# A chunked RWKV-7 recurrence under dense matmuls: turned keys made one step earlier and in another PSUM ring, six receptance buffers, a block inversion in less SBUF

## The chip, the cores and the metric

The kernel runs on one core of a Trainium2 chip. That core has a matrix engine (TensorE, here PE), a vector engine (VectorE, DVE), a scalar engine (ScalarE, ACT), a general engine (GpSimd, POOL) and a queue engine (SyncE, SP) that issues the DMAs. Each engine works through its own list of instructions in order and waits at semaphores for the others. The metric is the device time of one execution in microseconds (us); a lower one is better. Before the change the median of three runs is 2755.4 us (2751.41 to 2757.46).

## The reference

The program is a two-layer encoder trunk on one sequence of 1024 tokens with 1024 channels, all in float32:

- layer 0: RWKV-7 time mixing. Six shifted mixes of the input are projected (r, k, v, a decay, a rate a, a gate g). Per head of 64 channels (16 heads) a 64x64 state is carried over all tokens: `state = state*w + (state·a)⊗b + v⊗k`, and the output is `state·r`. Group norm per head, a bonus term, the gate and the output matrix `wo` follow.
- a layer norm of `alpha*x + f(x)`, then a squared-ReLU MLP (1024 to 4096 to 1024), and a layer norm again.
- layer 1: a diagonal complex state-space layer (S5) with GELU and a gated linear unit, layer norm, a second MLP, layer norm.

Only the recurrence of layer 0 is touched by the change.

## The kernel before

**Tiling.** The 1024 tokens are two halves H of 512. Dense layers keep activations as eight tiles of 128 channels x 512 tokens. Every dense product is made of three float32r matmuls (high x high, high x low, low x high; `mm3`), because each operand is split into a high and a low part (`split`: ACT casts, DVE subtracts). The results go to PSUM tiles named `d`. In what follows a *block matmul* is one matmul into a `d` tile, most of them 128x512.

**The recurrence.** It is computed in chunks of 64 tokens by matmuls. There are eight units m = 0..7: unit m is half of the heads (q = m % 2) over 256 tokens, that is four chunks. A unit goes through

- `elem` (L488 on): loads r, k, decay and rate, makes the scaled receptances `AR` (tag `AR`, two tiles a unit, ring of `ARB` = 5) and scaled keys `KB` (two tiles, ring of 2), with small matmuls `pss`, `pn`, `pb` into the PSUM ring `a` (pool `pa`, two buffers);
- `amat` (L563): 32 matmuls `pA` of `KB` with `AR`, also into ring `a`, which DVE masks into the chunk matrices `AT`;
- `kbtrans` (L586): the keys turned, 16 transposes on PE into four PSUM tiles `pT` of ring `c` (pool `pc`, two buffers), which ACT copies to four tiles `kbt` (ring of `KTB` = 4, all of them one unit's);
- `invert` (L598): inverts the unit triangular 64x64 blocks of `AT`. ACT copies the diagonal 32x32 blocks to `blk`, DVE turns them into `xa` (L615), 30 pairs of small DVE instructions substitute forward in PSUM (`xh`), and 32 + 32 small matmuls `pv` with an ACT copy between them (L636, L640, L644) make the off-diagonal part. The result is `XT` (ring of 2);
- `chain` (L662): two halves of two chunks each. A chunk is a step of four matmul groups that wait for one another through ACT and DVE: `pR`, `pX`, `pU` (which uses `kbt`), `pO`. 32 steps make the whole sequence. `pR` to `pO` lie in ring `c`;
- `gnorm` (L713): group norm, bonus and gate, with four transposes `py` in ring `c`, and the store of y.

**Order.** All of it is one straight program. `core` (L767) gives each part a rank, and a list scheduler places the instructions of all engines by rank, by the readiness that it reckons with, and by free buffers. The result is a fixed list per engine. Block matmuls of the projections, of `wo(0)` and of the first MLP have late ranks and fill PE between the steps of the recurrence. A ring of two buffers means that a third tile's first writer waits until the first tile's last reader is done.

**Around it.** `rwkv_proj(0)` and `rwkv_proj(1)` are the projections of the two halves, `wo(0)` follows, then the first layer norm (`layer_norm` from L829: column means `pm`, eight subtractions of `pm` from `hA` on DVE (L852), squares on ACT summed by DVE and POOL (L860), `pq`, the root in `rs` (L866, L867), `rb`, `pr`, eight products (L875), ACT, split). The MLP of half 0 can begin only behind that layer norm. `wo(1)` comes after twelve blocks of that MLP.

Of the kernel before, what the change touches and what calls it, by code (L numbers as in the profile page):

```python
# [33 lines left out]
LN8R = 400000  # L34
MIXR = 100
W0B = 5
ARB = 5
GB = (2, 3, 4)
GV = True

AEN = (0, 0, 0, 0)
# [29 lines left out]
def trunk(ctx, tc, A):  # L71
# [513 lines left out]

    def kbtrans(D):  # L586
        D.kbt = {}
        for j in range(2):
            for c2 in range(2):
                p = pc.tile([128, 2, 2, 128], F32, tag="c", name="pT")  # L590
                for cc in range(2):
                    for i in range(2):
                        PE.transpose(p[:, cc, i], D.KB[j][:, 4 * i + 2 * c2 + cc].rearrange("p j l -> p (j l)"), ident)
                t = kp.tile([128, 2, 2, 128], F32, tag="kbt", name="kbt", bufs=KTB)
                S.copy(t, p)
                D.kbt[j, c2] = t

    def invert(D):  # L598


        at = D.at
        xa = kp.tile([128, 32, 32], F32, tag="xa", name="xa", bufs=1)
        x1 = kp.tile([128, 2, 16, 32], F32, tag="x1", name="x1", bufs=1)
        tmp = x1[:, 0].rearrange("p u j -> p (u j)")
        blk = x1[:, 1]

        xh = pl.tile([128, HT], F32, tag="l", name="xh")
        xv = xh.rearrange("p (t j) -> p t j", t=32)
        xt = kp.tile([128, 16, L], F32, tag="XT", name="XT", bufs=2)
        D.xt = xt  # L610
        for h in range(2):
            for q in range(2):
                r = slice(64 * h + 32 * q, 64 * h + 32 * q + 32)
                S.copy(blk[r].rearrange("p (c i) j -> p c i j", i=NP), at[r, h, :, :, 0, 32 * q : 32 * q + 32])
        V.transpose(xa.rearrange("p t (e u) -> p t e u", e=2),  # L615
                    blk.rearrange("p u t -> p t u").unsqueeze(2).broadcast_to([128, 32, 2, 16]))

        S.mul(xv, xa[:, :, 0:32:2], emask[:, 0:1])
        V.scalar_tensor_tensor(xv, xa[:, :, 1:32:2], emask[:, 1:2], xv, op0=ALU.mult, op1=ALU.add)
        for s in range(1, 31):  # L620
            nt, w = 31 - s, (s + 1) // 2
            tv = tmp[:, 0 : nt * w].rearrange("p (t j) -> p t j", t=nt)
            V.tensor_mul(tv, xa[:, s + 1 : 32, s : s + 1].broadcast_to([128, nt, w]),
                         xv[:, s : s + 1, 0:w].broadcast_to([128, nt, w]))
            V.tensor_add(xv[:, s + 1 : 32, 0:w], xv[:, s + 1 : 32, 0:w], tv)
        for e in range(2):
            d = xh[:, 16 * e : 16 * e + 496 : 33]
            V.tensor_scalar(d, d, emask[:, e : e + 1], None, op0=ALU.add)
        V.transpose(x1[:, 0].rearrange("p u (j e) -> p j e u", e=2), xv.rearrange("p t j -> p j t"))
        V.transpose(xt.rearrange("p u (e t) -> p u e t", e=2),  # L630
                    x1[:, 0].unsqueeze(2).broadcast_to([128, 16, 2, 32]))
        pv1 = pl2 = pl.tile([128, HT], F32, tag="l", name="pv1").rearrange("p (u j) -> p u j", u=16)
        for u in range(16):
            for h in range(2):
                r0 = 64 * h
                PE.matmul(pv1[r0 + 32 : r0 + 64, u], at[r0 : r0 + 32, h, u // NP, u % NP, 0, 32:64],  # L636
                          x1[r0 : r0 + 32, 0, u], start=True, stop=True)
        for h in range(2):
            r0 = 64 * h
            S.copy(x1[r0 + 32 : r0 + 64, 0], pv1[r0 + 32 : r0 + 64])  # L640
        for u in range(16):
            for h in range(2):
                r0 = 64 * h
                PE.matmul(pl2[r0 : r0 + 32, u], x1[r0 + 32 : r0 + 64, 0, u],  # L644
                          xt[r0 + 32 : r0 + 64, u, 32:64], start=True, stop=True)
        for h in range(2):
            r0 = 64 * h
            S.copy(xt[r0 : r0 + 32, :, 32:64], pl2[r0 : r0 + 32])
            G.memset(xt[r0 + 32 : r0 + 64, :, 0:32], 0.0)

        for j in range(2):
            for h in range(2):
                hs = slice(64 * h, 64 * h + 64)
                (S.copy if AEN[2 * j + h] == 0 else G.tensor_copy)(
                    at[hs, h, :, 2 * j : 2 * j + 2, 0], D.AR[j][hs, :, 0].rearrange("p (i c) l -> p c i l", i=2))
# [116 lines left out]
    def core():  # L772
# [5 lines left out]
            cur = elem(0)  # L778
        with rank(5000):
            amat(cur)  # L780
            invert(cur)
        with rank(100000):
            run(pg)
        last = None
        for m in range(8):
# [7 lines left out]
                with rank(LN1R):  # L793
                    first_out.append(layer_norm(first_out[0], 0, 0))
            base = m * 10000
            with rank(base + RK[0]):
                kbtrans(cur)
            nxt = None
            if m < 7:
                with rank(base + RK[1]):  # L800
# [9 lines left out]
            if nxt and m < 6:  # L810
                with rank(base + RK[3]):
                    amat(nxt)
            with rank(base + RK[4]):
                chain(cur, 1)
            with rank(base + RK[5]):
                gnorm(cur, 0)
            if nxt:
                with rank(base + RK[6]):
                    if m == 6:
                        amat(nxt)  # L820
                    invert(nxt)
            last, cur = cur, nxt
        with rank(base + 8000):
# [556 lines left out]
```

## Time and profile before

| | before |
|---|---|
| median of three runs | 2755.4 us (2751.41 to 2757.46) |
| the profiled execution's own time | 2756.91 us |
| its span, first to last instruction | 2755.1 us |
| PE busy | 2602.8 us, 94% of the span |
| DVE / ACT / POOL busy | 1811.4 / 1156.3 / 628.2 us |
| mean granted TensorE clock | 0.958 |
| DMA, bytes moved | 345.90 MB |

Times in the profile are microseconds, engines are named as above, and L12 is line 12 of the kernel before. "Idle before" is how long an engine stood still ahead of an instruction, with what ended that wait behind an arrow. PEclk is the share of full speed that the chip granted to TensorE: 1.0 is 2.4 GHz and 0.5 is 1.2 GHz. Matmuls overlap in the records, so the step from one start to the next tells more of their cost than the duration.

### The profile page before, as it was taken

The page shows a single profiled execution, that of the slowest core. Times are in us where ns is not written, and L with a number is a line of the kernel's source. Part 1 is how long each engine was busy: PE and PEld are TensorE (multiplying, and loading weights), DVE is VectorE, ACT ScalarE, POOL GpSimd, SP SyncE. Part 2 cuts the span into 40 slices and gives each one's busy share as a digit, 9 for nine tenths or more (in the row PEclk, how much of TensorE's full clock was granted, in tenths as well). Part 3 has the DMA queues.
Part 4 walks back from the last instruction along what each step waited for, and adds up shares of the span by engine and source line. Part 5 has one row for each costly group of instructions (what it writes and reads, how often), then busy time and mean ns, then how long its engine had stood idle before and what let it go on. Part 6 is the DMA issues. An engine that isn't in the chain of part 4 may idle for free.

```text
span 2755.1 us, 43773 instructions
## 1 busy us (share of the span) xinstructions
PE 2602.8 (94%) x16582; PEld 2099.3 (76%) x16582; DVE 1811.4 (66%) x3191; ACT 1156.3 (42%) x2038; POOL 628.2 (23%) x515
## 2 busy tenths in 40 slices
PE   7999879899899999889999999999999999999997
PEld 5778767678777877667877788778778887788886
DVE  7477676477788767997658554574765546855556
ACT  7455574554453333344432332344223324433333
POOL 3120642341334212332122000120220001210101
PEclk9989979899879999999999999999999999999999
DMA  4765455465222334564233533233343332333333
GB/s 146 234 206 164 153 180 153 148 192 170 87 79 83 99 94 145 138 157 140 89 123 118 185 96 98 83 89 106 113 164 112 98 96 85 115 96 97 97 94 103
DMA packets 215058, 345.90 MB, mean 126 GB/s; under 512 B 21184, under 2 KB 75584, under 8 KB 214848
## 3 DMA queue, kind: packets, MB, share of 16 engines
q1 hardware_dynamic: 214848, 343.10, 40.2%
q8 instruction: 131, 2.15, 0.3%
q14 instruction: 79, 0.65, 0.1%
HBM read 279.06 MB, written 63.96 MB: 125 GB/s over the span
## 4 chain that ended last, share of the span: by engine, by line
PE 63%; DVE 12%; DMA 5%; issue 4%; ACT 2%; POOL 1%; SPq 0%; ACTq 0%; DVEq 0%; POOLq 0%
PE d L188 53%; DVE wlo L149 2%; DMA wraw<-in_mw_dram 2%; PE py L1234 1%; PE pA L580 1%; PE py L1239 1%; DMA yl<-s_y 1%; DVE hA L975 1%; PE pbu L1190 1%; PE pu L154 1%; PE pR L687 1%; PE pX L692 0%; POOL rl L959 0%; ACT whi L148 0%; DVE t L1202 0%
## 5 line engine op out<-in xcount | busy, mean ns | idle before, releaser
L148 ACT CAST whi<-wraw 128x512 fp32r<-128x512 f32 x668 | 413.6, 620 | 932.0 <-PE d L188 625.0
L149 DVE TENSOR_TENSOR wlo<-wraw,whi 128x512 fp32r<-128x512 f32 x668 | 497.8, 746 | 432.6 <-ACT whi L148 412.7
L188 PE MATMUL d<-qbuf,whi 128*128 128x512 f32 (+1 forms) x2112 | 655.0, 393 | 20.5 <-DVE hA L975 7.7
L188 PEld LDWEIGHTS d<-qbuf,whi 128*128 128x128 f32 x2112 | 390.7, 190 | 115.2 <-DVE hA L975 14.6
L188 PE MATMUL d<-qbuf,wlo 128*128 128x512 f32 (+1 forms) x1056 | 409.5, 390 | 9.5 <-DVE wlo L149 9.3
L188 PE MATMUL d<-oAh,whi 128*128 128x512 f32 (+1 forms) x960 | 394.4, 414 | 21.0 <-ACT ev L417 8.4
L959 POOL TENSOR_TENSOR rl<-rl 128x512 f32<-128x512 f32 x128 | 155.7, 1216 | 1084.4 <-ACT rl L958 1080.4
L188 PE MATMUL d<-oAl,whi 128*128 128x512 f32 (+1 forms) x960 | 390.6, 408 | 5.6 <-DVE oAl L149 5.6
L188 PE MATMUL d<-oAh,wlo 128*128 128x512 f32 (+1 forms) x960 | 390.2, 407 | 5.8 <-DVE wlo L149 3.4
L188 PE MATMUL d<-oBh,whi 128*128 128x512 f32 x704 | 278.6, 396 | 0.0
L188 PE MATMUL d<-oBh,wlo 128*128 128x512 f32 x704 | 277.7, 395 | 0.0
L188 PE MATMUL d<-oBl,whi 128*128 128x512 f32 x704 | 276.4, 393 | 0.0
L188 PEld LDWEIGHTS d<-qbuf,wlo 128*128 128x128 f32 x1056 | 200.0, 190 | 55.1 <-DVE wlo L149 13.6
L188 PEld LDWEIGHTS d<-oAh,whi 128*128 128x128 f32 (+1 forms) x960 | 188.0, 196 | 66.5 <-ACT ev L417 10.2
L188 PEld LDWEIGHTS d<-oAh,wlo 128*128 128x128 f32 (+1 forms) x960 | 188.2, 196 | 49.9 <-DVE wlo L149 5.1
L188 PEld LDWEIGHTS d<-oAl,whi 128*128 128x128 f32 (+1 forms) x960 | 188.4, 196 | 46.9 <-DVE oAl L149 7.8
L975 DVE TENSOR_TENSOR hB<-hB,d 128x512 f32<-128x512 f32 (+1 forms) x256 | 165.2, 651 | 70.7 <-PE d L188 67.9
L975 DVE TENSOR_TENSOR hA<-hA,d 128x512 f32<-128x512 f32 x240 | 162.3, 683 | 47.1 <-PE d L188 44.2
L188 PEld LDWEIGHTS d<-oBh,wlo 128*128 128x128 f32 x704 | 132.5, 188 | 32.1 <-issue 2.0
L188 PEld LDWEIGHTS d<-oBl,whi 128*128 128x128 f32 x704 | 132.6, 188 | 29.9 <-issue 0.9
L188 PEld LDWEIGHTS d<-oBh,whi 128*128 128x128 f32 x704 | 132.8, 189 | 28.2 <-issue 0.7
L149 DVE TENSOR_TENSOR qbuf<-rl,qbuf 128x512 fp32r<-128x512 f32 x128 | 95.7, 748 | 73.0 <-ACT qbuf L148 72.6
(373 smaller groups left out, 3818.1 us busy)
## 6 DMA issues: line engine op xcount, KB each, us to landing
wraw<-in_mw_dram SPq DMA_DIRECT2D x520, 256.0 KB, 2.7
wraw<-in_glu_dram SPq DMA_DIRECT2D x64, 256.0 KB, 2.6
low<-wlo SPq DMA_DIRECT2D x52, 256.0 KB, 2.7
wlo<-low SPq DMA_DIRECT2D x52, 256.0 KB, 3.5
wraw<-in_wk_dram SPq DMA_DIRECT2D x32, 256.0 KB, 3.6
wraw<-in_wr_dram SPq DMA_DIRECT2D x32, 256.0 KB, 3.6
wraw<-in_wv_dram SPq DMA_DIRECT2D x32, 256.0 KB, 4.2
yl<-s_y SPq DMA_DIRECT2D x32, 256.0 KB, 3.1
```

The source lines that it names most:

```text
L148: S.copy(hi, src)
L149: (e or V).tensor_sub(lo, src, hi.bitcast(F32))
L154: PE.matmul(out, x, idt, start=True, stop=True)
L188: bulk.append((PE.matmul(p, w, x, **kw).ins, x.shape[-1]))
L580: PE.matmul(pp[h][:, cc, i], D.KB[j][hs, u].rearrange("p j l -> p (j l)"), D.AR[j][hs, u].rearrange("p j l -> p (j l)"), start=True, stop= ...
L687: hop.append(PE.matmul(pR[hs, i], at[:, h, c, i, 0], vsa[:, cl, h, i], start=True, stop=True))
L959: G.tensor_mul(r, r, r)
L975: V.tensor_add(z, z, p)
L1190: PE.matmul(p[qs, g2, ri], tb[:, g2, ri, qs], u[:, 2 * g2 + par], start=True, stop=True)
L1234: PE.matmul(p[64 * j : 64 * j + 64, g2], ug[f][:, 2 * g2 + par], tv[:, par, g2], start=g2 == 0, stop=False, skip_group_check=True)
L1239: PE.matmul(p[64 * j : 64 * j + 64, g2], hb[qs, 4 * f + g2, ri, 0:NSC], tcm[qs, g2, ri], start=False, stop=ri == 1, skip_group_check=True)
```

## The change

Four things are edited.

1. `kbtrans` is called for the *next* unit, right behind its `amat`, with a rank of `base + 2500`; before, it was called for the current unit at the top of the loop. Its PSUM tiles come from ring `a` and no longer from ring `c`, and its loops run over the chunk pair first.
2. `ARB` goes from 5 to 6.
3. `GB` becomes empty: `gnorm(last, 1)` is traced behind `chain(cur, 0)` for all units, where it was traced ahead of it for m = 2, 3, 4.
4. In `invert` the tile `xa` (4 KB in each partition) goes; the first turned form lies in the unit's own `XT` tile, which is now taken at the beginning of the inversion. `blk` and `tmp` share one tile of 2 KB where `x1` had 4 KB.

An `AR` tile has 4 KB in each partition, so the SBUF use falls by 2 KB.

```diff
-ARB = 5
-GB = (2, 3, 4)
+ARB = 6
+GB = ()
...
     def kbtrans(D):
         D.kbt = {}
-        for j in range(2):
-            for c2 in range(2):
-                p = pc.tile([128, 2, 2, 128], F32, tag="c", name="pT")
+        for c2 in range(2):
+            for j in range(2):
+                p = pa.tile([128, 2, 2, 128], F32, tag="a", name="pT")
...
-        xa = kp.tile([128, 32, 32], F32, tag="xa", name="xa", bufs=1)
-        x1 = kp.tile([128, 2, 16, 32], F32, tag="x1", name="x1", bufs=1)
-        tmp = x1[:, 0].rearrange("p u j -> p (u j)")
-        blk = x1[:, 1]
+        x1 = kp.tile([128, 16, 32], F32, tag="x1", name="x1", bufs=1)
+        tmp = x1.rearrange("p u j -> p (u j)")
+        blk = x1
...
         xt = kp.tile([128, 16, L], F32, tag="XT", name="XT", bufs=2)
         D.xt = xt
+        xa = xt.rearrange("p u j -> p (u j)").rearrange("p (t j) -> p t j", t=32)
...
         with rank(5000):
             amat(cur)
+            kbtrans(cur)
             invert(cur)
...
-            with rank(base + RK[0]):
-                kbtrans(cur)
             nxt = None
...
             if nxt and m < 6:
                 with rank(base + RK[3]):
                     amat(nxt)
+                with rank(base + 2500):
+                    kbtrans(nxt)
...
                 with rank(base + RK[6]):
                     if m == 6:
                         amat(nxt)
+                        kbtrans(nxt)
                     invert(nxt)
```

The scheduler makes another order of it on every engine. From the last step of the recurrence on, the lists of all engines are the same again. Three places in the lists follow, each as the program lists it (line, operation, written tile, read tiles, shape, and how many stand in a row). In the changed kernel the lines of `invert`, `chain` and `gnorm` are shifted by one, those of the layer norm by three.

PE at the first layer norm, before: from the second `pm` matmul (the mean, with the last of the eight columns) on. `pn`, `pb`, `pR` to `pO` and `pA` are the recurrence, and `pq` is the layer norm's sum of squares.

```order
L850 MATMUL pm<-hA,ones_c 128x512
L528 MATMUL pn<-ident,sq 128x128 x4
L557 MATMUL pb<-rksel,kf 64x1 x10
L687 MATMUL pR<-vsa,AT_7087 64x64 x8
L557 MATMUL pb<-rksel,kf 64x1 x6
L692 MATMUL pX<-o,XT 64x64 x8
L580 MATMUL pA<-AR,KB 128x128 x8
L697 MATMUL pU<-vsa,kbt 64x64 x8
L706 MATMUL pO<-st,AR 64x64 x8
L708 MATMUL pO<-vsa,AT_7087 64x64 x8
L580 MATMUL pA<-AR,KB 128x128 x3
L864 MATMUL pq<-ones_c,sq_7814 128x1
```

And PE at the same place of the changed program:

```order
L853 MATMUL pm<-hA,ones_c 128x512
L580 MATMUL pA<-AR,KB 128x128
L593 MATMUL pT<-ident,KB 128x128 x4
L580 MATMUL pA<-AR,KB 128x128 x3
L688 MATMUL pR<-vsa,AT_7082 64x64 x8
L593 MATMUL pT<-ident,KB 128x128 x4
L693 MATMUL pX<-o,XT 64x64 x8
L593 MATMUL pT<-ident,KB 128x128 x8
L698 MATMUL pU<-vsa,kbt 64x64 x8
L707 MATMUL pO<-st,AR 64x64 x8
L709 MATMUL pO<-vsa,AT_7082 64x64 x8
L520 MATMUL pss<-hsel,sq 128x2
```

Twenty-eight of the 32 `pA` of a unit have moved to the front of the layer norm, among the block matmuls of `wo(0)`; four are left behind the mean, and the unit's 16 `pT` now stand there.

DVE at the same layer norm, before: from the eight subtractions of the mean on.

```order
L852 TENSOR_TENSOR hA<-hA,pm 128x512 x8
L529 TENSOR_TENSOR kk<-kk,pn 128x512
L734 TENSOR_REDUCE vr<-osq 128x8
L559 COPY bo<-pb 128x2x4
L860 TENSOR_TENSOR sq_7814<-sq_7814,sq 128x512
L693 COPY vsa<-pX 64x256
L546 SCALAR_TENSOR_TENSOR AR<-kk,E 128x8x64
L735 TENSOR_SCALAR vr<-vr 128x8
L860 TENSOR_TENSOR sq_7814<-sq_7814,sq 128x512
L551 TENSOR_TENSOR KB<-lda,ldsg 64x8x64 x2
L583 TENSOR_TENSOR AT<-pA,amask 128x2x256 x2
L860 TENSOR_TENSOR sq_7814<-sq_7814,sq 128x512
```

And DVE at the same place of the changed program:

```order
L855 TENSOR_TENSOR hA<-hA,pm 128x512 x8
L583 TENSOR_TENSOR AT<-pA,amask 128x2x256
L863 TENSOR_TENSOR sq_7836<-sq_7836,sq 128x512
L694 COPY vsa<-pX 64x256
L550 TENSOR_TENSOR KB<-kf,ldsg 64x8x64 x2
L863 TENSOR_TENSOR sq_7836<-sq_7836,sq 128x512
L616 STREAM_TRANSPOSE XT<-x_8413 128x1024
L863 TENSOR_TENSOR sq_7836<-sq_7836,sq 128x512
L701 TENSOR_TENSOR st<-pU,st 128x256
L702 TENSOR_TENSOR st<-st,PL 128x256
L729 TENSOR_REDUCE sm<-o 128x8
L730 TENSOR_SCALAR sm<-sm 128x8
```

Before, fourteen more instructions stand between the last of these rows and the one that writes `rs` (L866): two state updates, a copy of the state, a scan, a receptance product, a copy, two `AT` products and the rest of two group norms. In the changed program three stand there (L731, L764, L522).

PE at the end of the r projection of half 1, before: `pv` (L636, L644) is the off-diagonal part of an inversion, `pss` and `pn` are the two matmul groups of the key norm. The first fence is at the gate (unit 2's inversion), the second at the values of half 1 (unit 4).

```order
L636 MATMUL pv_3585<-x_3511,AT 32x32 x32
L593 MATMUL pT<-ident,KB 128x128 x8
L644 MATMUL pv_3585<-XT,x_3511 32x32 x32
L593 MATMUL pT<-ident,KB 128x128 x2
L557 MATMUL pb<-rksel,kf 64x1 x16
L520 MATMUL pss<-hsel,sq 128x2 x3
```

```order
L520 MATMUL pss<-hsel,sq 128x2 x4
L593 MATMUL pT<-ident,KB 128x128 x4
L762 MATMUL py<-ident,o 128x2x64 x4
L188 MATMUL d<-oAh,whi 128x512
L188 MATMUL d<-oAl,whi 128x512
L188 MATMUL d<-oAh,wlo 128x512
L528 MATMUL pn<-ident,sq 128x128 x4
L557 MATMUL pb<-rksel,kf 64x1 x16
```

And PE at these two places of the changed program:

```order
L637 MATMUL pv_3610<-x_3536,AT 32x32 x32
L580 MATMUL pA<-AR,KB 128x128 x4
L188 MATMUL d<-oAh,wlo 128x512
L188 MATMUL d<-oAh,w2st 128x512
L580 MATMUL pA<-AR,KB 128x128 x4
L688 MATMUL pR<-vsa,AT 64x64 x5
L580 MATMUL pA<-AR,KB 128x128 x4
L645 MATMUL pv_3610<-XT,x_3536 32x32 x32
L688 MATMUL pR<-vsa,AT 64x64 x3
L580 MATMUL pA<-AR,KB 128x128 x16
```

```order
L580 MATMUL pA<-AR,KB 128x128 x8
L188 MATMUL d<-oAh,whi 128x512
L188 MATMUL d<-oAl,whi 128x512
L188 MATMUL d<-oAh,wlo 128x512
L580 MATMUL pA<-AR,KB 128x128 x4
L593 MATMUL pT<-ident,KB 128x128 x16
L188 MATMUL d<-whi,oAh 128x256
```

The transposes that stood between the two `pv` groups are replaced by `pA`, two block matmuls and part of a `pR`. At the second place `pss` and `pn` are no longer three block matmuls apart, and all 16 `pT` of a unit stand in one piece behind its last `pA`.

## Rows read from the trace of the kernel before

**Rows 1.** The page's first part: busy time, share of the span, instructions

```profile
PE 2602.8 (94%) x16582; PEld 2099.3 (76%) x16582; DVE 1811.4 (66%) x3191; ACT 1156.3 (42%) x2038; POOL 628.2 (23%) x515
```

**Rows 2.** Busy time in three stretches: PE, PEld, DVE, ACT, POOL, PEclk, DMA

```profile
95.00:850.00 755.00, 687.22 (x6229) 569.34 (x6230) 530.27 (x1077) 395.58 (x734) 254.76 (x207) 0.88 0.49 153
740.00:780.00 40.00, 30.99 (x249) 26.44 (x247) 37.08 (x55) 17.18 (x33) 24.93 (x20) 0.56 0.22 66
850.00:1050.00 200.00, 199.51 (x1532) 159.83 (x1533) 141.24 (x266) 73.68 (x138) 41.95 (x36) 1.00 0.31 96
```

**Rows 3.** Waits of PE, 0 to 1050 us: total us, times, longest

```profile
PE pA L580 <- DVE AT L583: 6.4, 3, 3.3
PE pn L528 <- ACT sq L525: 5.1, 3, 3.0
PE pv L644 <- ACT x L640: 3.6, 1, 3.6
PE pb L557 <- POOL kf L552: 3.4, 5, 1.8
PE pT L593 <- ACT kbt L595: 1.0, 1, 1.0
```

**Rows 4.** Timeline of PE at the layer norm: start us, us, engine, line

```profile
722.93 0.60 PE L593 MATMUL pT<-ident,KB 128*128 128x128 f32 x4
723.29 0.49 PE L188 MATMUL d<-oAh,whi 128*128 128x512 f32 x1
...
743.07 0.68 PE L692 MATMUL pX<-o,XT 64*64 64x64 f32 x16 [0.34 <-ACT o L689]
746.12 3.09 PE L580 MATMUL pA<-AR,KB 64*128 64x128 f32 x16 [2.37 <-DVE kk L529]
...
778.49 1.22 PE L188 MATMUL d<-oAh,whi 128*128 128x512 f32 x2 [0.91 <-ACT oAh L148]
```

**Rows 5.** Timeline of DVE at the layer norm

```profile
740.60 4.87 DVE L852 TENSOR_TENSOR hA<-hA,pm 128x512 f32<-128x512 f32 x8 [0.36 <-PE pm L850]
...
746.65 1.31 DVE L860 TENSOR_TENSOR sq<-sq,sq 128x512 f32<-128x512 f32 x1
...
752.08 1.38 DVE L551 TENSOR_TENSOR KB<-lda,ldsg 64x512 f32<-64x512 f32 x2
753.49 1.29 DVE L583 TENSOR_TENSOR AT<-pA,amask 128x512 f32<-128x512 f32 x2
...
762.76 0.69 DVE L730 TENSOR_TENSOR o<-o,sm 128x512 f32<-128x512 f32 x1
...
765.36 0.16 DVE L866 TENSOR_SCALAR rs<-pq 128x4 f32<-128x4 f32 x1
...
773.21 4.87 DVE L875 TENSOR_TENSOR hA<-hA,pr 128x512 f32<-128x512 f32 x8 [0.17 <-PE pr L872]
```

**Rows 6.** Timeline of POOL at the layer norm

```profile
746.15 1.26 POOL L547 TENSOR_TENSOR lda<-kk,lda 128x512 f32<-128x512 f32 x1 [0.73 <-DVE kk L529]
...
780.98 1.65 POOL L523 TENSOR_TENSOR rn<-rn,mhalf 128x8 f32<-128x8 f32 x1
```

**Rows 7.** Tiles xa and kbt: duration ns min/median/max, first and last start

```profile
L615 DVE STREAM_TRANSPOSE xa<-x x8: 1934/2034/2120, 155.5 to 931.3; 128x1024 f32<-128x1024 f32 x8
L595 ACT COPY kbt<-pT x32: 567/587/597, 182.5 to 922.7; 128x512 f32<-128x512 f32 x32
```

**Rows 8.** Timeline of PE where half 1's values begin

```profile
589.35 0.66 PE L528 MATMUL pn<-ident,sq 128*128 128x128 f32 x4 [3.02 <-ACT sq L525]
```

**Rows 9.** All waits of the span: total us, times, longest

```profile
DVE AR L545 <- DMA ldr<-s_r: 22.4, 8, 6.4
```

**Rows 10.** Tiles oBh and st: first users, last step; columns as in rows 7

```profile
L188 PE MATMUL d<-oBh,whi x704: 387/394/632, 1133.5 to 2701.3; 128*128 128x512 f32 x176
L706 PE MATMUL pO<-st,AR x512: 218/218/366, 257.2 to 1046.1; 64*64 64x64 f32 x171
```

More of the change, by code (lines that the diff above doesn't have):

```diff
@@ L628, in invert @@
             V.tensor_scalar(d, d, emask[:, e : e + 1], None, op0=ALU.add)
-        V.transpose(x1[:, 0].rearrange("p u (j e) -> p j e u", e=2), xv.rearrange("p t j -> p j t"))
+        V.transpose(x1.rearrange("p u (j e) -> p j e u", e=2), xv.rearrange("p t j -> p j t"))
         V.transpose(xt.rearrange("p u (e t) -> p u e t", e=2),
-                    x1[:, 0].unsqueeze(2).broadcast_to([128, 16, 2, 32]))
+                    x1.unsqueeze(2).broadcast_to([128, 16, 2, 32]))
         pv1 = pl2 = pl.tile([128, HT], F32, tag="l", name="pv1").rearrange("p (u j) -> p u j", u=16)
@@ L636, in invert @@
                 PE.matmul(pv1[r0 + 32 : r0 + 64, u], at[r0 : r0 + 32, h, u // NP, u % NP, 0, 32:64],
-                          x1[r0 : r0 + 32, 0, u], start=True, stop=True)
+                          x1[r0 : r0 + 32, u], start=True, stop=True)
         for h in range(2):
             r0 = 64 * h
-            S.copy(x1[r0 + 32 : r0 + 64, 0], pv1[r0 + 32 : r0 + 64])
+            S.copy(x1[r0 + 32 : r0 + 64], pv1[r0 + 32 : r0 + 64])
         for u in range(16):
@@ L643, in invert @@
                 r0 = 64 * h
-                PE.matmul(pl2[r0 : r0 + 32, u], x1[r0 + 32 : r0 + 64, 0, u],
+                PE.matmul(pl2[r0 : r0 + 32, u], x1[r0 + 32 : r0 + 64, u],
                           xt[r0 + 32 : r0 + 64, u, 32:64], start=True, stop=True)
```

## The prediction

> **What bounds the kernel now.** I read the page first: PE is busy for 94% of the span, DVE for 66% [rows 1]. So PE sets the time, and a change that neither adds nor takes away matmuls (13293 in either list) can only move PE's waits and its clock. The table of stretches then says where there is anything to move. From 850 to 1050 us PE is busy for 199.51 of 200 us at a clock of 1.00. From 95 us, shortly before the two lists begin to differ, to 850 us it is busy for 687 of 755 us at 0.88 [rows 2]: 68 us of waiting and some 90 us of clock lie there. The recurrence ends at 1046.1 us. Its result is first needed by PE at 1133.5 us [rows 10], and in the changed list the last step stands 35 block matmuls later (3021 against 2986 ahead of it), about 8 us, so that end has 87 us of room and costs nothing. From there on the lists are the same. The whole difference must come from the waits of PE before 850 us.
>
> The waits of PE [rows 3] show what the recurrence itself leaves open: `pA` for the masking by DVE, `pn` and `pb` for the key norm, the second `pv` group for ACT, `pT` for its copy. The worst single place is in the table of stretches: 740 to 780 us, clock 0.56, PE busy for 31 of 40 us with slow small work, while DVE is busy for 37 of 40 [rows 2]. That is the first layer norm. No block matmul can run until it is done, and DVE is its limit.
>
> **The change part by part.**
>
> *The layer norm.* The timeline of DVE starts the eight subtractions at 740.60 and writes `rs` at 765.36, 24.8 us later. The first product stands at 773.21, and the next block matmul of PE at 778.49 [rows 4, 5]: 37.9 us in all. In DVE's list of the changed program there are fewer foreign instructions ahead of `rs`. I sum them by these rows: 4.87 for the subtractions; 0.65 for one masking (half of 1.29); three sums of squares at 0.69, 2.07; the two key products 1.38; the turning of the blocks 2.03 [rows 7]; six instructions of at most 128x512 (`vsa`, two of `st`, one sum, one difference, one product with the gate) at 0.69 or less, 4.14; two tiny ones at 0.16, 0.32. That is 15.5 us, 9.3 less [rows 5]. The longest sum of squares took 1.31 [rows 5], which would add 1.9. Behind `rs` I give back nothing: before, 7.85 us pass to the first product. In the changed list the chain from `rn` over POOL (1.65), `kk` (0.69), POOL (1.26) and the key products (1.38) stands ahead of that product, 5.0 us and two hops over ACT and PE [rows 5, 6]. So the gap becomes 28.6 us.
>
> What left the gap still has to be done, now among block matmuls at full clock. 28 `pA` go (8 take 3.09 us at half clock, so 5.4 us at full), and a `pR` and a `pX` group (0.68 each); 16 `pT` come in (0.36 us for four, from the step of 722.93 to 723.29) and one `pss` group, which I set at the same 0.36 [rows 4]. That makes 5.4 + 1.4 - 1.8 = 5.0 us. The layer norm thus brings -9.3 + 5.0 = **-4.3 us**. The bounds: +5.0, if the squares on ACT and POOL and not DVE's list hold `rs` where it is, and -9.3, if the moved matmuls all fall into waits that PE has anyway (68 us of them).
>
> *The places where a consumer stood too close.* `pn` waited 3.02 us because `pss` stood three block matmuls ahead of it [rows 8]; in the changed list the same pair is 32 narrower block matmuls apart. The longest `pb` wait (1.8) came in such a pair too, in another unit. The `pv` wait of 3.6 came with only eight `pT` (0.72 us) between the groups; there are now twelve `pA` (2.3), two block matmuls (0.5) and five `pR` (0.4) there, 3.2 of the 4.3 us needed, so 1.1 stay. Gone: 3.0 + 1.8 + 3.6 = 8.4 us [rows 3, 4]. New: two waits of `pT` at the sixteen in a row, by the one such row 1.0 each; one wait of `pA` where sixteen stand in a row, by the mean of its row 2.1; the 1.1 from above. Together 5.2. Net **-3.2 us**, between -8.4 (no new wait) and +8 (five new waits of the longest `pA` kind, 3.3 each, less the 8.4).
>
> *The ring.* A `pT` now takes one of the two buffers that `pss`, `pn`, `pb` and `pA` use. Its copy on ACT (0.587 us [rows 7]) needs one of four `kbt` tiles, which a chunk of the running unit has to free with its `pU`. So the third and fourth `pT` of a unit can hold both buffers for one or two steps. In the changed list this shows as a later `elem`: the first `pss` of unit 4 stands behind 1327 block matmuls instead of 1240. That `elem` has time: the steps of unit 4 start 10 block matmuls earlier all the same. I cost it at nothing. If the cover goes, it is the ring rival below. The Trainium skill, PSUM — Partial Sum Buffer, "Engine vs sequencer instructions", says that matmuls start and complete in program order. By that rule a `pT` without a free buffer holds back every block matmul behind it, where by DVE's and ACT's idle time alone it would cost nothing. The trace agrees: at 589.35 a `pn` stood for 3.02 us with block matmuls behind it [rows 8].
>
> *The rest.* A sixth receptance buffer: no row of the waits shows the receptances waiting for a reader, they wait for their load (22.4 us, 8 times [rows 9]), so 0, and at most one such wait, 6.4, of DVE and not of PE. The inversion in `XT` and one `x1`: the same instructions on one in-order engine, and the `XT` of two units back is long read; 0, and if not, a turning (2.03 [rows 7]) late in a unit whose chain waits for nothing. Two `kbt` copies now stand ahead of the copy of the state on ACT in some steps: 1.17 us against the 0.8 that DVE needs there anyway, hidden by the block matmuls between `pU` and the next `pR`. `gnorm` traced later: no instruction more or less, its places are in the sums.
>
> **Sum.** -4.3 - 3.2 = -7.5 us. The profiled execution took 2756.9 us (span 2755.1 and 1.8 around it), so 2749.4; it lies 1.5 above the median of the runs, so 2747.9. Forecast: **2748 us**, 0.27% less.
>
> **Rivals.**
>
> *It only moves (2753 us).* 9.3 us of DVE work leave the layer norm and land at 700 to 740 us, ahead of the low halves of weights for block matmuls. For it: the products of `pA` and the group norm come just where the weights of `wo(0)` are split. Against: DVE is busy for 530 of 755 us in this stretch [rows 2], so there is room. If five of the 9.3 us are met by PE, -7.5 becomes -2.5 and the median 2753.
>
> *The ring holds PE (2766 us, slower).* Seven units of the eight have two places each where the third and fourth `pT` or the `pA` behind them wait for a buffer. Price of one: the mean of the four such waits before, (6.4 + 1.0) / 4 = 1.85 us [rows 3]. For it: two buffers served three users before and serve four now, and sixteen `pT` in one piece are more than the ring holds. Against: of the waits of PE only 7.4 us in 850 were of this kind. From five places on (9.2 us) the gain is gone; ten of the fourteen give 18.5 - 7.5 = +11, 2766 us; all of them 2774.
>
> *The gap is not shortened.* If the squares hold `rs` (three sums on POOL and a product there between), the layer norm costs +5.0 instead of -4.3: 2757 us. It counts to the no-change case.
>
> **How the numbers follow.** A measurement of this kernel can tell a change from none at about 0.2%, 5.5 us: below 2750 is faster, above 2761 slower. Forecast 0.52, which also holds everything below it. Only moved or not shortened, 2750 to 2761: 0.26. The ring: 0.22. The bounds of the terms, -9.3 and -8.4 on one side, +5.0 and +8 on the other, reach from 2738 to 2768; a few us more below come from a shorter stretch at half clock (40 us at 0.56 lose 17.6 us; a quarter less is 4). I take 2734 to 2764: it leaves out the ring with more than nine places, and little below. The forecast's own range is 2734 to 2750.
>
> **What would show it.** In the profile after: from the first subtraction of the mean to the first matmul of the MLP 25 to 31 us instead of 37.9, with `rs` 14 to 18 us behind it; no wait of `pn` over 2 us; a `pv` wait near 1; PE busy with the same 2600 us or slightly less where the clock is higher. Wrong: a line of waits of `pT` or `pA` over 10 us together (the ring), a new wait of block matmuls for `wlo` or `oAl` before 740 us (only moved), or `rs` still 24 us behind the first subtraction.

## The result, and the profile after

The changed kernel takes 2761.88 us, the median of 20 runs (2747.54 to 2781.75), against 2751.97 for the kernel before in the same batch (20 runs, 2739.82 to 2760.35): a ratio of 1.0044 with a 95% interval of 1.003 to 1.0059 (the quotient of the two medians is 1.0036). That is slower by 10 to 12 us where 7.5 us less were forecast. Its profiled execution took 2763.13 us. In four later batches the medians of the kernel before were 2746.2 to 2749.4 us, so the execution that the forecast started from (2756.9) was itself 5 to 11 us above the usual. All ratios below are against the kernel before of the same batch.

The page of the kernel after, the line that answers to [rows 1]:

```profile
PE 2615.0 (95%) x16582; PEld 2103.3 (76%) x16582; DVE 1807.9 (65%) x3191; ACT 1157.1 (42%) x2038; POOL 628.3 (23%) x515
```

PE has as many instructions as before, but is busy for 12.2 us longer. As no matmul was added, that is clock, or records that overlap less. The stretches of [rows 2] in the kernel after, and one of 27.6 us between (length, then busy us of PE, PEld, DVE, ACT, POOL, then the clock, the DMA share and GB/s):

```profile
95.00:850.00 755.00, 689.46 (x6051) 565.06 (x6050) 519.64 (x1073) 387.81 (x718) 248.44 (x204) 0.88 0.49 152
400.00:427.60 27.60, 27.60 (x245) 23.62 (x244) 15.00 (x21) 18.63 (x32) 4.99 (x6) 0.51 0.29 91
740.00:780.00 40.00, 29.71 (x295) 21.88 (x297) 33.11 (x50) 17.11 (x34) 18.12 (x14) 0.78 0.26 76
850.00:1050.00 200.00, 200.00 (x1599) 160.10 (x1598) 140.93 (x256) 79.17 (x146) 43.72 (x38) 1.00 0.32 93
```

Up to 850 us PE gets through 178 matmuls fewer than before (6051 against 6229) at the same clock and no less busy. So the loss lies there, where the gain was to lie. (At 740 to 780 us the two kernels are no longer at the same work, so that row says little by itself.) The waits of PE up to 1050 us, as [rows 3] (total us, times, longest; `...` stands for rows left out):

```profile
...
PE pm L852 <- DVE sa L850: 6.6, 1, 6.6
...
PE d L188 <- DMA wlo<-low: 5.4, 3, 4.2
PE d L188 <- DVE wlo L149: 5.4, 6, 1.9
...
PE pss L520 <- ACT kbt L595: 3.6, 1, 3.6
PE pT L593 <- ACT kbt L595: 3.0, 3, 1.5
...
PE pA L580 <- DVE bo L559: 2.8, 2, 1.8
...
PE pn L528 <- ACT sq L525: 2.0, 1, 2.0
...
PE pb L557 <- POOL kf L552: 1.4, 1, 1.4
```

The `pn` and `pb` waits shrank as forecast (5.1 and 3.4 before), the one of 3.6 us between the `pv` groups is gone, and `pT` and `pA` are no queue. The longest single wait of the small matmuls is one that no term had: the first mean of the layer norm (0.3 before). New too are the 3.6 us of `pss` behind a `kbt` copy, a wait for a buffer of ring `a`. And block matmuls wait longer for the low halves of weights (`wlo`): 5.4 us in each of the two rows shown, 2.7 and 2.9 before. The timeline of DVE there, after, the rows that answer to [rows 5]:

```profile
746.96 1.75 DVE L849 TENSOR_TENSOR sb<-sb,hA 128x512 f32<-128x512 f32 x1
748.74 0.69 DVE L850 TENSOR_TENSOR sa<-sa,sb 128x512 f32<-128x512 f32 x1
...
768.83 4.87 DVE L855 TENSOR_TENSOR hA<-hA,pm 128x512 f32<-128x512 f32 x8 [0.49 <-PE pm L853]
...
786.71 0.16 DVE L869 TENSOR_SCALAR rs<-pq 128x4 f32<-128x4 f32 x1 [2.42 <-PE pq L867]
...
792.06 4.87 DVE L878 TENSOR_TENSOR hA<-hA,pr 128x512 f32<-128x512 f32 x8
```

And PE in the same stretch (as [rows 4]):

```profile
749.48 2.07 PE L852 MATMUL pm<-sa,ones_c 128*128 128x512 f32 x2 [6.58 <-DVE sa L850]
751.48 1.22 PE L580 MATMUL pA<-AR,KB 64*128 64x128 f32 x4
752.63 1.11 PE L763 MATMUL py<-ident,o 128*128 128x128 f32 x4
...
794.87 1.22 PE L188 MATMUL d<-oAh,whi 128*128 128x512 f32 x2 [0.93 <-ACT oAh L148]
799.18 0.80 PE L188 MATMUL d<-oAl,whi 128*128 128x512 f32 x1 [3.09 <-DVE oAl L149]
```

The row of before that answers to the last one, right behind the last of [rows 4]:

```profile
779.91 0.80 PE L188 MATMUL d<-oAl,whi 128*128 128x512 f32 x1 [0.20 <-DVE oAl L149]
```

From the first subtraction to `rs` 17.9 us pass (24.8 before), to the first matmul of the MLP 26.0 (37.9 before, 28.6 forecast). So the gap that the forecast measured did close. But PE had stood for 6.58 us ahead of it, behind the mean of the first seven columns, with small `pA` and `py` behind that. And two matmuls into the MLP it stands again, for 3.09 us (0.20 before), for the low half `oAl`. Up to that third matmul 30.4 us pass, 39.3 before: 9.0 us less, not 11.9.

### The profile page after: what moved, and what is told of

It reads as the page before. It is cut to its first block, busy times and chain, and to the rows that moved or that the text cites. A ratio compares the mean times of both kernels' runs of the same rounds, so it can differ in the third digit from the quotient of the medians.

```text
span 2761.4 us, 43796 instructions
## 1 busy us (share of the span) xinstructions
PE 2615.0 (95%) x16582; PEld 2103.3 (76%) x16582; DVE 1807.9 (65%) x3191; ACT 1157.1 (42%) x2038; POOL 628.3 (23%) x515
## 4 chain that ended last, share of the span: by engine, by line
PE 45%; issue 3%; DVE 3%; DMA 1%; POOL 1%; ACT 1%; SPq 0%; ACTq 0%; DVEq 0%; POOLq 0%
PE d L188 40%; PE py L1237 1%; PE py L1242 1%; DMA wraw<-in_mw_dram 1%; POOL rl L962 1%; PE pu L154 1%; DVE wlo L149 1%; PE pbu L1193 1%; ACT whi L148 0%; PE pu L1182 0%; PE pq L867 0%; PE pu L156 0%; DMA tt<-tT 0%; DVE hB L978 0%; DVE t L1205 0%
## 5 line engine op out<-in xcount | busy, mean ns | idle before, releaser
L188 PEld LDWEIGHTS d<-qbuf,whi 128*128 128x128 f32 x2112 | 391.1, 190 | 114.7 <-DVE hA L978 12.5
L188 PE MATMUL d<-oAl,whi 128*128 128x512 f32 (+1 forms) x960 | 392.4, 410 | 5.0 <-DVE oAl L149 4.9
```

Source lines behind the costliest of these rows:

```text
L188: bulk.append((PE.matmul(p, w, x, **kw).ins, x.shape[-1]))
```

## The experiments

A number in what follows needs a word. "Block matmul 1250" is the 1250th matmul into a `d` tile on PE, counted in a trace from the start; places in the program's lists, as 2118, 2337 and 2512 below, are five lower than that count. Stretch A runs from block matmul 1250 to 2100, stretch B (with the first layer norm) from 2100 to 2500.

### Which of the four edits

Each edit was taken back, or done, alone. In these four expectations theory 1 is that the early turned keys in ring `a` cost, theory 2 that `GB` or the sixth buffer does, theory 3 that the parts don't add up.

`a_kbt_back`: the changed kernel with the turned keys at their old place and in ring `c`.

```diff
-                p = pa.tile([128, 2, 2, 128], F32, tag="a", name="pT")
+                p = pc.tile([128, 2, 2, 128], F32, tag="c", name="pT")
...
+            with rank(base + RK[0]):
+                kbtrans(cur)
...
-                with rank(base + 2500):
-                    kbtrans(nxt)
```

> The changed kernel with the turned keys put back: called at the top of the loop for the running unit, in ring c; ARB 6, GB empty and the smaller inversion stay. Theory 1 (the early turned keys in ring a cost the time): back to the kernel before, 0.997 to 1.001 of it, 2744 to 2755 us. Theory 2 (GB or the sixth receptance buffer costs it): stays at 1.003 to 1.006, 2760 to 2768. Theory 3 (no part by itself; each new list has other waits and another clock): anywhere from 0.997 to 1.006, without the parts adding up.

`b_only_kbt`: the kernel before with the turned keys alone moved (the reverse of that diff; `ARB` 5, `GB` (2, 3, 4), the old inversion).

> The kernel before with the turned keys alone moved to ring a behind the next unit's chunk matrices; ARB 5, GB (2, 3, 4) and the old inversion stay. Theory 1: 1.003 to 1.006, 2760 to 2768 us, with PE's clock between 100 and 850 us at 0.88 or lower. Theory 2: 0.998 to 1.002. Theory 3: anywhere from 0.997 to 1.006.

`d_gb_back`: the changed kernel with `GB = (2, 3, 4)`.

> The changed kernel with GB (2, 3, 4) again. Theory 1: as the changed kernel, 1.003 to 1.006. Theory 2 with GB as the cause: 0.998 to 1.002. Theory 3: anywhere between, and the wait of the layer norm's first mean for DVE (6.6 us in the changed kernel) may go without the time going back.

`e_arb5`: the changed kernel with `ARB = 5`.

> The changed kernel with five receptance buffers. Theory 1: as the changed kernel, 1.003 to 1.006. Theory 2 with the sixth buffer as the cause (units run further ahead and their small matmuls pile up): 0.998 to 1.002. Theory 3: anywhere between.

| | ratio to before | 95% | median us |
|---|---|---|---|
| turned keys taken back | 1.0010 | 0.9998 to 1.0023 | 2750.2 |
| only turned keys moved | 0.9944 | 0.9925 to 0.9964 | 2731.9 |
| `GB` (2, 3, 4) again | 0.9954 | 0.9934 to 0.9973 | 2736.9 |
| `ARB` 5 again | 1.0041 | 1.0026 to 1.0056 | 2757.2 |

The sixth buffer is worth nothing (1.0041 against 1.0044; PE's list is the same). The smaller inversion is worth nothing either: the second and third row differ in it and in `ARB`, have the same list on PE, and agree within their intervals. Two edits are left. The early turned keys alone gain 0.56%, so theory 1 is wrong. The empty `GB` without the early keys costs 0.1%, within the interval nothing (first row), but on top of the early keys 0.9 to 1.0%: theory 2, and a part of theory 3, because it costs only together.

### Which unit's group norm

`GB` names the passes m of the unit loop in which the second group norm of unit m-1 is traced ahead of the next chunks. With the early turned keys, all eight choices were run; the edit is the one line `GB = ...`. In the first four expectations theory 1 is unit 3, theory 2 the half-clock cluster at 400 us (unit 1), theory 3 a share of each, theory 4 chance; in the last two A is the late norms as such, B the landing at the layer norm, C chance.

> The changed kernel with GB = (4,): only the second group norm of unit 3 is traced ahead of the chunks of unit 4 again; those of units 1 and 2 stay behind. On TensorE its y transposes stand at place 1525 instead of 1944, and the first mean's matmuls at 2133 instead of 2118; the cluster of small matmuls at places 1165 to 1189 stays as in the changed kernel. Theory 1 (the group norm of unit 3 is what costs: its y late, the chunk matrices of units 6 and 7 in front of the layer norm, TensorE made to wait for the first mean): all of the 1.0% comes back, 0.994 to 0.997 of the kernel before, no wait of 6.6 us in front of the first mean. Theory 2 (the cluster at 400 us costs: 27 us at half clock, set by the group norm of unit 1): no change, 1.003 to 1.006. Theory 3 (each has a share): about half, 0.998 to 1.001. Theory 4 (each list lands by chance): no rule.

> The changed kernel with GB = (2, 3): the other half, the second group norms of units 1 and 2 are traced ahead of the next unit's chunks again, that of unit 3 stays behind. The cluster of small matmuls at places 1165 to 1189 is broken up as in the list with GB = (2, 3, 4); the y transposes of unit 3 stay late, at place 1959. Theory 1 (unit 3): no change against the changed kernel, 1.003 to 1.006 of the kernel before, with a wait in front of the first mean. Theory 2 (the cluster, unit 1): 0.994 to 0.997, with some 10 us at half clock instead of 27 between 395 and 440 us. Theory 3 (shares): 0.998 to 1.001. Theory 4: no rule.

> The changed kernel with GB = (2,): only the second group norm of unit 1 ahead again. The cluster at places 1165 to 1189 is broken up; unit 3's y transposes at 1959. Theory 1 (unit 3): 1.003 to 1.006. Theory 2 (the cluster, unit 1): 0.994 to 0.997. Theory 3 (shares): the cluster's share alone, (27.3 - 10.2) / 2 = 8.5 us, 1.000 to 1.002. Theory 4: no rule.

> The changed kernel with GB = (3,): only the second group norm of unit 2 ahead again. The cluster at places 1165 to 1189 stays, unit 3's y transposes stay late (1956), the places between 1365 and 1480 go back, the first mean stands at place 2131. Theories 1, 2 and 3 all give no more than the 5 us that the 10 us at half clock between places 1434 and 1474 can cost: 1.002 to 1.006. Theory 4 (chance): anything from 0.994 to 1.006; a time under 1.000 here speaks for it, or for the first mean's place alone.

> The changed kernel with GB = (3, 4): second group norms of units 2 and 3 ahead of the next chunks, that of unit 1 behind. Measured alone they gave 0.9949 (unit 2) and 0.9995 (unit 3) against 1.0044 with neither. If the effects add: 0.990, the fastest of all. If one of them is enough (theory B, the layer norm lands well or it doesn't; first mean at 2130): 0.994 to 0.997. Theory C (chance): as likely at 0.999, as GB = (2, 3) came out, as at 0.995.

> The changed kernel with GB = (2, 4): units 1 and 3 ahead, unit 2 behind; the one place of the eight combinations that tells whether unit 2 is needed. Theory A with unit 2 as the one that decides: 1.000 to 1.004. Theory B (first mean at 2130): 0.995 to 1.000. If the effects add (unit 1 nothing, unit 3 half a per cent): 0.9995. Theory C: no rule.

| `GB` | ratio | 95% | `GB` | ratio | 95% |
|---|---|---|---|---|---|
| () | 1.0044 | 1.003 to 1.0059 | (2, 3) | 0.9989 | 0.9975 to 1.0003 |
| (2) | 1.0040 | 1.0027 to 1.0052 | (2, 4) | 0.9977 | 0.9963 to 0.9991 |
| (3) | 0.9949 | 0.993 to 0.9967 | (3, 4) | 0.9971 | 0.9953 to 0.999 |
| (4) | 0.9995 | 0.9983 to 1.0006 | (2, 3, 4) | 0.9954 | 0.9934 to 0.9973 |

Unit 3 alone gives back half, unit 2 alone all of it, both together no more than unit 2 alone. No sum of shares makes that table; theories 1 to 3 are out. The cluster at 400 us is out in another way as well. The kernel with `GB = (3)` stands at half clock there for 37.5 us and is among the fastest (its stretch from 388.6 us on, columns as above):

```profile
388.60:426.10 37.50, 35.68 (x290) 29.60 (x291) 22.86 (x41) 24.49 (x44) 9.64 (x9) 0.50 0.33 108
```

### The same late norms in another list

`k_2700` keeps `GB` empty and changes only the rank of the turned keys; `lgb2` keeps it empty too and gives the sixth buffer's room to a second log-gate tile.

```diff
-                with rank(base + 2500):
+                with rank(base + 2700):
                     kbtrans(nxt)
```

```diff
-ARB = 6
+ARB = 5
-LGB = 1
+LGB = 2
```

> The changed kernel with GB = () as it is; only the rank of the next unit's turned keys is 2700 behind the base instead of 2500. The list is another one from unit 4 on: unit 3's late y transposes stand at place 1961, the first mean's matmuls at 2130 instead of 2118 with 3 block matmuls behind them instead of 15. Theory A (group norms traced behind the next chunks cost 1% by themselves): 1.003 to 1.006 of the kernel before. Theory B (what costs is how the list lands at the layer norm, with TensorE made to wait there for the first mean): no such wait, 0.994 to 1.000. Theory C (half per cent steps by chance of the list): anything between 0.994 and 1.006, and the profile shows the difference to the changed kernel mainly as time at half clock.

> The changed kernel with GB = () as it is, five receptance buffers instead of six (which changed nothing) and, in the room of the sixth, a second buffer for the group norm's log-gate tile (LGB 2). The late norms of units 1 and 3 stand where they stood or later (y transposes of unit 3 at 1961), the first mean at 2130 with 3 block matmuls behind it; the list of the layer norm reads as with the rank of 2700. Theory A: 1.003 to 1.006. Theory B: 0.994 to 1.000, and within 0.2% of the kernel with the rank of 2700. Theory C: no rule, also between these two.

Ratios 0.9994 (0.9978 to 1.001) and 0.9977 (0.9958 to 0.9995). So late norms do not cost 1% as such (theory A is wrong): a rank that brings no norm forward takes half of it back. In both, PE's waits of the layer norm read otherwise. For the first, from 440 to 910 us:

```profile
PE pA L580 <- DVE AT L583: 9.3, 4, 4.7
...
PE pm L853 <- DVE hA L946: 0.3, 1, 0.3
```

The wait at the mean is gone, but `pA` waits for DVE's masking instead (0.3 to 4.0 us there in three profiles of the changed list), so this does not show that the mean's wait was the cost. In the kernels with `GB` () and (2), the two slowest, PE stands instead for 6.6 us at the first mean or for 7.3 us at the `py` right ahead of it. With `GB` (2, 3) it is 2.4, with (3), (4), (2, 4) and (3, 4) 2.1 or less.

### The layer norm alone

`ln_late` is the changed kernel with another rank of the first layer norm; PE's list differs from the changed kernel's only between block matmuls 2118 and 2512. `gb_back_ln_late` is the same edit on `GB = (2, 3, 4)`; there the lists differ from 2118 to 2337. Theory D: the loss is made ahead of the layer norm.

```diff
-LN1R = -1
+LN1R = 62000
```

> The changed kernel with GB = () as it is; only the rank of the first layer norm goes from -1 to 62000. TensorE's list is that of the changed kernel up to block matmul 2118 and again from 2512 on; between, the first mean stands behind eight pA and the y transposes, not ahead of them. Theory B (TensorE, made to wait for the first mean with small work behind it, is what makes the changed kernel slow): the wait of 6.6 us goes, and with it the half clock that follows, 0.998 to 1.001 of the kernel before. Theory D (the loss is made ahead of the layer norm, in how the small work of units 2 to 5 is bunched between blocks): no change, 1.003 to 1.006, since nothing ahead of 2118 differs. If the lower rank only delays the subtractions: 1.005 to 1.008.

> The changed kernel with GB = (2, 3, 4) again (0.9954) and the rank of the first layer norm from -1 to 62000. TensorE's list is that of GB = (2, 3, 4) up to block matmul 2118 and again from 2337 on; between, two more matmul groups of a chain step, four y transposes and a pss group stand ahead of the last reduction of the layer norm. Theory B (the layer norm's landing decides): 5 to 13 us of the gain go, 0.997 to 1.000. Theory D (what stands ahead of the layer norm decides): 0.994 to 0.997.

`ln_late`: 1.0011 (0.9999 to 1.0023). So an order that differs in some 400 block matmuls around the layer norm is worth 0.33%, about 9 us. The wait did not vanish but changed its name: PE's timeline shows it in front of `py`, with the means behind it.

```profile
735.56 1.08 PE L763 MATMUL py<-ident,o 128*128 128x128 f32 x4 [6.68 <-DVE st L701]
737.30 2.07 PE L852 MATMUL pm<-sa,ones_c 128*128 128x512 f32 x2
...
779.20 1.22 PE L188 MATMUL d<-oAh,whi 128*128 128x512 f32 x2 [0.93 <-ACT oAh L148]
```

So the part of the expectation that named the wait as the cause failed, and only the place held. `gb_back_ln_late` came to 0.9960 (0.9943 to 0.9976), no change against 0.9954. There theory B had wanted a loss of 5 to 13 us and theory D none. B is true of the changed list at most, and not the whole of it: 0.57% more lie between `ln_late` and `GB = (2, 3, 4)`.

### Second profiles

Four kernels were profiled once more without timing, to see what of one profile belongs to the list.

> The changed kernel a second time, for its profile alone. Under theory B the layer norm's waits (6.6 us for the first mean) repeat, and the stretch from block matmul 2050 to 2200 takes 104 to 112 us as in the two profiles of this list. Under theory D the half clock between 395 and 430 us and at the block matmuls 1434 to 1474 repeats as well; if it doesn't, those places are the clock's chance in one execution.

> The kernel before with only the turned keys moved, a second time, for its profile alone. Expected: 97 to 98 us from block matmul 2050 to 2200 as in the two profiles of this list, and block matmul 2050 reached at 687 to 690 us. A start of that stretch later than 700 us would say that one profile can't place a difference of 10 us ahead of the layer norm.

> The kernel before a second time, for its profile alone. Its first profile took 2756.9 us, 5 to 11 us more than the medians of its timed runs, so the stage table of before is likely too slow somewhere. Theory E (the surplus is half clock ahead of the layer norm, by the chance of that one execution): the second profile reaches the first layer norm some 5 to 10 us earlier, with less time at half clock between 95 and 740 us. If the two profiles agree stage by stage, the surplus is the profiler's and all profiles carry it.

> GB = (3,) a second time, for its profile alone. Its first profile stood 37.5 us at half clock between 389 and 426 us, in the same cluster of small matmuls as the changed kernel, and was fast all the same. Theory E (how long that place stays at half clock is chance of one execution): another length here, anything from 10 to 37 us, and the time moves by half of the difference. If the list decides: 30 to 40 us again.

Their executions took 2758.95, 2738.99, 2748.97 and 2742.68 us. In the changed kernel the wait for the first mean came back (6.4 us), and so did the half clock at 400 us (26.1 us of it between 395 and 430 us, 29.2 in the first profile). With the turned keys alone, block matmul 2050 came at 691 us and 2200 another 98 us later, as expected within a microsecond. The sum of A and B comes back within 5.3 us for one list (A alone within 3.6), while the time to reach block matmul 1250 scatters by 10 us (450.3 and 440.1 in the kernel before). That is where the first profile of before had its surplus: theory E was right about the place, and the second profile begins the subtractions of the layer norm at 729.86 us and not at 740.60 [rows 5]. It was right about the clock in part only: up to block matmul 1250 the first profile has 6.9 us more of waits of PE, and 4.2 us more lost at half clock. The layer norm itself repeats (24.7 and 37.9 us in the second profile of before, 17.6 and 26.0 in that of the changed kernel). For `GB = (3)` theory E was wrong. The half clock there repeats:

```profile
385.70:423.20 37.50, 35.71 (x290) 29.63 (x291) 22.82 (x41) 24.48 (x44) 9.63 (x9) 0.50 0.32 110
```

Now the two stretches can be set side by side. The kernel before (second profile), A and then B:

```profile
440.10:708.40 268.30, 247.93 (x2384) 208.12 (x2383) 179.19 (x390) 131.94 (x246) 83.17 (x67) 0.94 0.52 164
708.40:888.70 180.30, 166.15 (x1413) 133.88 (x1412) 145.43 (x259) 79.46 (x150) 73.89 (x56) 0.87 0.28 86
```

The changed kernel (second profile):

```profile
443.80:726.10 282.30, 258.65 (x2528) 215.25 (x2526) 174.62 (x370) 137.59 (x259) 87.87 (x72) 0.92 0.52 164
726.10:898.40 172.30, 153.28 (x1198) 121.31 (x1197) 136.05 (x243) 71.10 (x132) 67.18 (x53) 0.89 0.26 81
```

Only the turned keys moved (second profile):

```profile
444.30:711.80 267.50, 250.11 (x2499) 209.65 (x2498) 174.62 (x366) 132.62 (x253) 85.54 (x69) 0.94 0.54 171
711.80:879.90 168.10, 154.63 (x1273) 124.05 (x1272) 137.33 (x251) 74.91 (x142) 75.32 (x55) 0.90 0.28 86
```

`ln_late`:

```profile
436.20:717.00 280.80, 258.73 (x2527) 214.37 (x2526) 173.69 (x369) 137.84 (x259) 87.49 (x71) 0.93 0.52 165
717.00:885.60 168.60, 149.95 (x1197) 119.39 (x1197) 134.00 (x242) 71.11 (x131) 65.53 (x51) 0.88 0.26 83
```

The sum of the two lengths orders these kernels as their timed ratios do. The next table splits it three ways: the idle time of PE (length less busy), the half-clock loss (half of PE's busy time at half clock, an estimate of what that time cost), and the rest, which is the work at full clock. The figures are means over the profiles of a list:

| list | profiles | A | B | A + B | idle | half-clock loss | rest | ratio |
|---|---|---|---|---|---|---|---|---|
| before | 2 | 270.1 | 178.8 | 448.9 | 33.7 | 37.1 | 378.1 | 1 |
| changed (two with `ARB` 6, one with 5) | 3 | 281.4 | 174.9 | 456.2 | 42.2 | 35.3 | 378.7 | 1.0044 |
| `ln_late` | 1 | 280.8 | 168.6 | 449.4 | 40.7 | 30.8 | 377.9 | 1.0011 |
| turned keys moved, `GB` (2, 3, 4) | 3 | 265.3 | 168.6 | 433.9 | 32.5 | 24.6 | 376.7 | 0.9944, 0.9954 |
| `GB` (3) | 2 | 273.9 | 160.6 | 434.5 | 34.6 | 24.6 | 375.3 | 0.9949 |

Over the twenty traces of before and of all the variants, A + B and the ratio go together with a correlation of 0.92. A and B alone don't, because a list that puts more small work ahead of block matmul 2100 has less behind it. One list doesn't fit: `GB = (2)`, at 1.0040, has an A + B of 447.4, less than before, with 44.2 us of waits and only 23.4 of half-clock loss; its profile is some 5 us longer behind B than the changed kernel's (1863.2 against 1857.9). And the rest runs from 370.9 to 383.7 over the twenty, so single lists can't be split to better than some microseconds.

The table says in which form the time comes and goes, not why. The early turned keys alone leave the waits about as they are (33.7 to 32.5) and save 12.5 us of half clock. The empty `GB` on top of them brings back 10.7 us of half clock and adds 9.7 us of waiting. Against the kernel before that makes 8.5 us more waiting, 1.8 less half clock and 0.6 more rest: 7.3 us of the 8.5 by which the profiled executions of the two differ on the mean (2761.5 against 2752.9).

## Why the prediction was wrong

**The step that failed** is one of the last: "`gnorm` traced later: no instruction more or less, its places are in the sums". Priced at nothing, it cost 25 us (1.0044 against 0.9954, two kernels that differ in it alone). It turned a change that gains 13 to 15 us into one that loses 10 to 12. The argument holds for work and not for order: PE's lists with `GB` empty and (2, 3, 4) differ from block matmul 1149 to beyond 2600, and the runs showed 9.7 us more of waits and 10.7 us more of half-clock loss in A and B in the place of nothing. That the result lies inside the wide range (2734 to 2764) is luck: the bounds that reach so far up were those of other terms.

**The layer norm, forecast at -4.3, came to about +5, by an estimate.** The gap did what was read off the lists: `rs` 17.9 us behind the first subtraction, inside the 14 to 18 given, and 26.0 us to the MLP. But the term began its count at the first subtraction on DVE. The bounding engine is PE, and PE was held 6.58 us ahead of that. Stretch B shortened by 3.9 us, and 8.9 us of small work (the rest of A alone, 231.6 to 240.5 us) moved out of it into A, which makes +5.0; B holds more than the layer norm, so this is rough. Behind `rs`, where the forecast left the time as it was, it even fell (8.2 us to the MLP, 13.1 before [rows 4, 5]), but 2.9 of these 5.0 us came back in the wait for `oAl` (3.09 against 0.20). The bound of +5.0 was the right end, for another reason than the squares. The rule of the Trainium skill that the forecast weighed at the ring (PSUM — Partial Sum Buffer, "Engine vs sequencer instructions": matmuls start and complete in program order) shows here: `pA`, whose operands no row shows late, stood behind the waiting mean for its 6.58 us.

**The too-close consumers, forecast at -3.2**, held in their parts: `pn` 2.0 at the longest, `pT` 1.5, the `pv` wait gone. Stretch A has 2.8 us more idle time all the same (20.5 to 23.3). It lies at the block matmuls, which wait 13.7 us there on the mean of three profiles, 11.0 before: the longest wait, 3.9 to 4.4 us in all three, is for the DMA of a low half, and 1.9 us, again in all three, for DVE's `wlo` at some 675 us. That last is the sign that the forecast gave for its rival "only moves", in small.

**The ring at nothing** was nearly right. `pT` and `pA` together wait 7.7 us, 7.4 before; the ring's one new price is the 3.6 us of `pss`. The kernels with the same ring and the old `GB` have that wait too (3.4 to 3.9 us) and are among the fastest. So the ring rival had nearly the right time (2766) by a mechanism that isn't what cost. The sixth buffer and the smaller inversion at nothing were right too.

**The clock was left out of the sum** but for "a few us more below". It is the largest single effect of the early keys: 12.5 us of half-clock loss less in A and B.

**A premise failed too.** The lists of PE are not the same behind the last step of the recurrence. In the traces the small `pk` and `pb` of layer 1 and the `pm`, `pq` and `pr` of the second half's layer norm stand between other block matmuls up to number 3700. From block matmul 2500 to 3750 the changed kernel takes 380.1 us on the mean of three profiles, the kernel before 377.9, so about 2 us of the loss lie where the forecast looked for none.

**What stays open.** Why `GB = (3)` is as fast as `(2, 3, 4)` and `(2, 3)` slower than both is not settled, nor why the early keys take half clock away and the late norms bring it back. The half clock at 400 us, ahead of A, isn't it: 27 to 34 us of it are there in all three profiles of the changed list, and yet it reaches block matmul 1250 at 445.4 us on the mean, where the turned keys alone reach it at 445.0. In stretch A one thing goes with the norm of unit 2: with early keys, block matmuls wait 3.2 to 8.0 us there in every profile whose `GB` holds 3, and 10.6 to 15.1 in every one without. But 0.9977 stands among the second group, so that is a part of the answer at most. An early place for the turned keys in ring `c` was not tried. No list found beats the kernel with the turned keys moved alone (2731.9 us); the second with `GB = (2, 3, 4)` agrees with it within the intervals.

## What to carry to other kernels

Where a list scheduler fills one bounding engine, an edit that only moves the trace order need not be free: among fourteen lists with the same matmuls, the time ran from 0.9944 to 1.0044 of before. Price it by an experiment of one line, and try it apart from the edits that were meant to gain. Count a gap from the last big instruction of the bounding engine to its next one, not from the first step of the engine that seems to hold it. Profile twice before reading differences of 10 us out of stretches, and compare stretches between the same instructions, not between the same microseconds.

## What the runs showed of the hardware

The clock of TensorE can stay at its lower level while the engine doesn't wait at all, and can do so in one execution of a list and not in another. The changed kernel at the place of the 27.6 us above, PE's timeline:

```profile
392.78 0.50 PE L188 MATMUL d<-oAh,whi 128*128 128x512 f32 x1 [3.11 <-ACT ev L410]
...
398.93 1.10 PE L557 MATMUL pb<-rksel,kf 64*64 64x1 f32 x32
399.96 0.53 PE L188 MATMUL d<-oAh,whi 128*128 128x512 f32 x1
...
400.85 1.92 PE L637 MATMUL pv<-x,AT 32*32 32x32 f32 x64
402.70 2.07 PE L580 MATMUL pA<-AR,KB 64*128 64x128 f32 x8
```

`ln_late`, whose list is the same here, and its clock from 390 to 430 us:

```profile
387.71 0.79 PE L188 MATMUL d<-oAh,whi 128*128 128x512 f32 x1 [4.21 <-ACT ev L410]
...
393.75 1.10 PE L557 MATMUL pb<-rksel,kf 64*64 64x1 f32 x32
394.78 0.50 PE L188 MATMUL d<-oAh,whi 128*128 128x512 f32 x1
...
395.44 1.20 PE L637 MATMUL pv<-x,AT 32*32 32x32 f32 x64
396.57 1.16 PE L580 MATMUL pA<-AR,KB 64*128 64x128 f32 x8
```

```profile
390.00:430.00 40.00, 36.63 (x462) 28.82 (x461) 33.05 (x66) 31.21 (x58) 12.15 (x12) 0.97 0.40 126
```

The same eight `pA` take 2.07 us in the one (granted clock 0.51, the 1.2 GHz level) and 1.16 in the other (0.97 between 390 and 430 us). Ahead of it PE had done `pn`, the 32 tiny `pb` and a few block matmuls in both, and before these it had waited for ACT in both (the first row of each fence). In the one the clock was down from 400.3 to 427.6 us; in the other it had been down around that wait, from 382.2 to 392.4 us, and was up behind it. The Trainium skill, TensorE: Matmul & The Clock Gate, "HAM oscillation — how this bites in real kernels", tells of the lower clock as what follows waits for DMA. No wait for a DMA is in this stretch: PE was busy for 27.60 of 27.60 us and the clock stayed down. The measurement decides here, and it doesn't say why one execution was at the lower level and the other not.
